# Four edits to a one-core hybrid-decoder kernel: sums of squares by split products with ones, w_o's sums in place, samples' decays weighted half a step sooner, the chunk rows' pool in reverse order

## The chip, the cores and the metric

The kernel runs on one core of one Trainium2 chip. The metric is the device time of the kernel in microseconds; a comparison uses the median of several runs. The engines are named as in the profile: PE (TensorE, the matrix engine) with its weight loads PEld, DVE (VectorE), ACT (ScalarE), POOL (GpSimd) and SP (SyncE, which here issues most of the DMAs). A name with q behind it (SPq, ACTq) is the instruction sequencer of that engine, where DMAs are issued.

## The reference, cut to what matters

One step of a decoder layer for a prompt of 1024 rows and 8 samples of 8 rows, 1088 rows together (T in the kernel):

```python
h = rmsnorm(x, norm_g) * (1 + scale[:, None]) + shift[:, None]
proj = h @ w_in
u_pool, z_pool, z_ssm, xbc, dt_raw, g_raw = jnp.split(proj, SPLITS, axis=-1)
p, pool_new = pool_mix(u_pool, pool_buf, pos0, pool_w, pool_scale)
p = (p * jax.nn.silu(z_pool)) @ w_pool_out
xbc_c, conv_new = causal_conv(xbc, conv_buf, conv_w, conv_b)
y, ssm_new = ssd(xs, dt, A, Bm, Cm, ssm_state)
y = (y + d_skip.astype(jnp.float32)[:, None] * xs).reshape(b, L, D_INNER)
y = rmsnorm(y * jax.nn.silu(z_ssm.astype(jnp.float32)), ssm_norm_g)
s = y.astype(x.dtype) @ w_ssm_out
gates = jax.nn.sigmoid(g_raw)
m = gates[..., :D_MODEL] * p + gates[..., D_MODEL:] * s
x = x + gate[:, None] * (m @ w_o)
```

and in the scan over chunks of 128 rows (`ssd`; the samples take one chunk of 8 rows each, from their own states):

```python
cb = jnp.einsum('bign,bjgn->bijg', Cq, Bq)
att = cb[..., None] * decay * dq[:, None]
y = jnp.einsum('bijge,bjgep->bigep', att, xq)
y = y + jnp.einsum('bign,bige,bgepn->bigep', Cq, jnp.exp(acs), h)
```

D_MODEL is 1024, D_INNER 2048 (DI), with four groups (g) of eight heads of 64 channels and a state of 128. The mean of squares inside the second `rmsnorm` (over the 2048 channels of y, for each row) is what the first of the four edits computes in another way.

## The kernel before, in words

Rows lie along the free axis and channels on the partitions, so a tile of 128 by 1088 holds 128 channels of all rows. A product in float32 is made of three products of split operands: `hi` is the rounded part, `lo` the rest, and hi*hi + hi*lo + lo*hi is summed in PSUM (the names `whi`, `wlo`, `yh`, `yl`). The program runs in stages.

1. Normalisation, the conditioning and the pairs of w_in columns. The pairs use one level of Strassen's scheme (`strassen`, `product`: matmul line L427, DVE additions L436 and L441, weight differences L364, splits on ACT L148 and POOL L151). Beside the last ten pairs runs `all_samples` (L1454 on), a generator that makes the samples' part of the scan, group by group, a step of it between two pieces of the pairs. A step ends at each `yield`.
2. The chunk stage, from about 797 to 1093 us: 32 chunks (four groups of eight, `chunk`), woven with the products by `ph` and by w_ssm_out (`products`, matmul line L235, DVE additions L1828 and L1849) and with `wo_splits`, which prepares w_o for a Strassen product at the end.
3. The tail from 1109 us: sums of squares, the products of the last group (`tail_unit`, `m_done`), and the last products with w_o.

**Order.** Within each engine the instructions run in program order, which the framework's scheduler sets by priorities, except that in the chunk stage PE's and SP's order is the one in which the code is written (`in_line`). So in that stage an edit of tiles or waits can move instructions on DVE, ACT and POOL, and not on PE and SP. Several names are rings: the third R tile of one use waits until the first of an earlier use is free; PSUM is split in rings too: PB for short results, and PA, of three banks, for the blocks of products (`GB`: 384, 352 and 352 rows).

**Samples.** For a group, `rows` scales x by dt into `xd`; `weigh` (L1345) multiplies C and B of all samples (matmul L1349), masks the product (DVE L1351) and multiplies the masked product with the decays into `dec` (DVE L1352); `spread` and `split` make the split operands of the state update (PE L1372, L1374; DVE L1376, L1382, L1385, L1386); `turn` transposes states (L1402); `within` multiplies `dec` with `xd` by the helper `inner` (matmul L1310) and adds D*x.

**Chunks.** Each chunk transposes x and B (L1610, L1612), multiplies B and C (L1613), copies B's transpose to `bt` (ACT L1615), scales x into `xd` (L1621) and `xw` (L1623, one buffer), weights `dec` and `cE` (L1628, L1630), and then multiplies: state update L1635, `inner` L1310 and L1313 (the latter from the state `hst`). `finish` squares the gated result and adds it to `sq_acc`, 128 by 1088, so that a sum over its 128 partitions is the sum of squares. The pool `ck` holds `bt`, `xd`, `xw`, `hst`, `ph` and `szs`; the first tiles asked for of it stand at its lowest addresses (L1814).

**w_o.** `wo_splits` loads for k = 0 to 3 two row blocks of 128 by 1024 of w_o (`up`, `dn`, DMAs L1892 and L1893), forms their differences and sums on DVE (L1900, L1901, L1904, L1905) and splits five results of 512 columns (`part`: ACT copy, POOL difference L1882; stores L1878 and, by `out`, L1887).

**Sums of squares.** For each of nine blocks of rows a matmul with a column of ones gives sums per row on the partitions (L1989); root and reciprocal follow there (L1991, L1992). To bring the result back along the free axis on all partitions, each block becomes a diagonal matrix (DVE L1997) that is multiplied by ones (L1998) into three PSUM banks `rstd`. `m_done` multiplies the gate row tile `r` by them in three pieces (L2047).

Of the kernel before, what the change touches and what calls it, by code (L numbers as in the profile page):

```python
# [46 lines left out]
def tile_pool_ssd_step(  # L47
# [43 lines left out]
    def R(shape=(P, T), dt=F32):  # L91
        return hs.tile(list(shape), dt, tag="R", name=nm("R"), bufs=3)
# [4 lines left out]
    def PB():  # L97
        return psB.tile([P, 512], F32, tag="ps", name=nm("ps"))
# [1351 lines left out]
    def all_samples():  # L1450
# [8 lines left out]
        gs_[0].spread(0)  # L1459
        yield  # L1460
        gs_[0].split(0)
        yield
        for g, m in enumerate(gs_):
            n = gs_[g + 1] if g + 1 < NG else None
            if g:
                gs_[g - 1].end(1)
            m.weigh()
            m.turn(0)
            m.turn(1)
            m.turned(0)  # L1470
# [53 lines left out]
            m.out()  # L1524
            m.update(6)
            m.update(7)
            yield
        gs_[-1].end(1)
        yield
# [281 lines left out]
    cl = open_("cl", 2)  # L1811
    right = tc.tile_pool(name="ck", bufs=2, side="right", reuse_waits="tile")
    ck = right.__enter__()
    for shape, tag, bufs in (((P, 512), "ph", 3), ((P, 512), "hst", 2), ((P, 4, NS), "szs", 1)):  # L1814
        ckt(shape, tag, bufs)

    sq_acc = hs.tile([P, T], F32, tag="sq", name="sq_acc", bufs=1)
# [57 lines left out]
    def wo_splits():  # L1875
# [20 lines left out]
        yield  # L1896
        for k in range(4):
            up, dn = got
            su = R()
            WOE.tensor_tensor(su[:, left_], dn[:, right_], up[:, right_], ALU.subtract)  # L1900
            WOE.tensor_tensor(up[:, right_], up[:, right_], up[:, left_], ALU.subtract)  # L1901
            out()
            yield
            WOE.tensor_tensor(su[:, right_], su[:, left_], up[:, left_], ALU.add)  # L1904
            WOE.tensor_tensor(dn[:, right_], su[:, right_], dn[:, left_], ALU.subtract)  # L1905
            part(oT1, k, up[:, right_])
            yield
            out()
            part(oB11, k, up[:, left_])
            part(oT4, k, dn[:, right_])  # L1910
            yield
            out()
            part(oT3, k, su[:, left_])
            yield
            if k < 3:
                got = rows(k + 1)
            out()
            part(oT2, k, su[:, right_])
            yield
        out()  # L1920
        yield
# [60 lines left out]
        return mp.tile([P, 4, 512], F32R, tag=name, name=name, bufs=1)  # L1982


    rs9 = rs
    ps = PB()
    for c in range(9):
        n = min(P, T - c * P)
        mm(ps[:n, c:c + 1], sq_acc[:, c * P:c * P + n], ones[:, 0:1], start=True, stop=True)  # L1989
    for n, c in ((P, slice(0, 8)), (NS, slice(8, 9))):  # L1990
        act(rs9[:n, c], ps[:n, c], AF.Sqrt, bias=eps[:n], scale=1.0 / DI)  # L1991
        V.reciprocal(rs9[:n, c], rs9[:n, c])  # L1992
    rstd = [PB() for _ in range(3)]
    for c in range(9):
        n = min(P, T - c * P)
        dg = sm.tile([P, P], F32, tag="stc", name=nm("dg"), bufs=4)[:n, :n]
        V.tensor_scalar(dg, ident[:n, :n], rs9[:n, c:c + 1], None, ALU.mult)  # L1997
        mm(rstd[c // 4][:, c % 4 * P:c % 4 * P + n], ones[:n, :], dg, start=True, stop=True)  # L1998

    lo_, up_ = slice(0, 512), slice(512, 1024)
    a11h, a11l, s3h, s3l, s1h, s2h = [part4(n) for n in ("a11h", "a11l", "s3h", "s3l", "s1h", "s2h")]
# [37 lines left out]
    def m_done(m):  # L2042
        r = R()
        load(r, gs_d[m])
        for j, ps in enumerate(rstd):
            s = slice(512 * j, min(512 * j + 512, T))
            V.tensor_tensor(r[:, s], ps[:, :s.stop - s.start], r[:, s], ALU.mult)  # L2047
        mt = M()
        load(mt, m1_d[m])
        a = acc[m]  # L2050

        def done(o, n, ps):
            s = slice(o, o + n)
            V.tensor_tensor(a[:, s], ps[:, :n], a[:, s], ALU.add)
            if m < 7:
                s = slice(0, T)
                if o + n < T:
                    return
            V.tensor_tensor(a[:, s], a[:, s], r[:, s], ALU.mult)
            V.tensor_tensor(a[:, s], a[:, s], mt[:, s], ALU.add)  # L2060
        return done
# [262 lines left out]
```

## Time and profile before

| what | value |
|---|---|
| runs (3) | 1259.56, 1262.73, 1265.03 us; median 1262.73 |
| profiled execution, its own time | 1257.42 us |
| its span in the profile | 1255.7 us |
| mean granted clock of PE | 0.999 |
| PE busy | 1237.1 us, 99% |
| DVE busy | 964.7 us, 77% |
| ACT busy | 671.2 us, 53% |
| POOL busy | 715.3 us, 57% |
| DMA | 257.53 MB, mean 205 GB/s |

A row of a timeline gives the start in us from the start of the span, how long the piece took, the engine, the source line and operation, the tiles written and read, the shape, how many instructions are taken together, and in brackets the idle time just before with what ended it. Matmuls overlap, so the time of a row of several is not the distance to the next row: the distance between two starts is what they cost. A row of the waits names the engine and line that waited, what for, and then the total in us, how often, and the longest. A row of a line gives the number of instructions and the shortest, middle and longest duration in ns. A row of windows gives, for a stretch, the busy time of PE, PEld, DVE, ACT and POOL in this order, each with its number of instructions, then PE's clock, the DMA share and GB/s.

### The profile page before, as it was taken

The numbers are of one execution on the slowest core, as the hardware profiler recorded it, in microseconds if no ns is written. First come the engines' busy times: TensorE is split into PE (matmuls) and PEld (weight loads), VectorE is DVE, ScalarE is ACT, GpSimd is POOL, SyncE is SP. The second block draws the span as 40 slices with busy tenths as digits, with TensorE's granted clock in tenths as the row PEclk, the third lists the DMA queues.
The fourth block names the chain that finished last, engine by engine and source line by source line (L and its number), as shares of the span: only waits on it lengthen the run. The fifth ranks groups of instructions, "written<-read, shape, count | busy, mean of one in ns | idle before, by whom it ended". The sixth has DMA issues, their size and how long they took to land.

```text
span 1255.7 us, 26515 instructions
## 1 busy us (share of the span) xinstructions
PE 1237.1 (99%) x9733; PEld 1159.4 (92%) x9733; DVE 964.7 (77%) x1709; ACT 671.2 (53%) x1542; POOL 715.3 (57%) x607
## 2 busy tenths in 40 slices
PE   9999999999999999999999999999999999999997
PEld 8889999999999999999999999989888888999885
DVE  6993888877988688886666665588677888659986
ACT  6864366555656566546444443656676656402425
POOL 1137768775968677654443334355576777503662
PEclk9999999999999999999999999999999999999999
DMA  9946355474546544435566564998788877866884
GB/s 321 314 139 214 118 177 182 138 223 136 182 155 203 164 153 158 160 112 155 149 188 179 161 197 142 329 310 277 239 249 271 288 242 250 284 228 216 247 197 156
DMA packets 262715, 257.53 MB, mean 205 GB/s; under 512 B 27993, under 2 KB 202345, under 8 KB 262578
## 3 DMA queue, kind: packets, MB, share of 16 engines
q1 hardware_dynamic: 181856, 163.49, 42.5%
q10 hardware_dynamic: 78426, 88.16, 20.3%
q0 software_dynamic: 2304, 4.20, 1.9%
q8 instruction: 77, 1.26, 0.4%
q14 instruction: 52, 0.43, 0.1%
HBM read 170.80 MB, written 85.10 MB: 204 GB/s over the span
## 4 chain that ended last, share of the span: by engine, by line
PE 65%; DVE 3%; DMA 2%; POOL 1%; issue 1%; ACT 1%; SPq 0%; DVEq 0%; POOLq 0%; ACTq 0%
PE mm L235 16%; PE mm L427 14%; PE ps L427 14%; PE ps L1310 2%; PE pc L427 2%; PE pc L1635 2%; PE ps L1313 2%; PE ps L2119 2%; PE ps L2121 2%; PE ps L2120 2%; PE ps L1402 1%; DMA xb<-xbc 1%; PE ps L1425 1%; PE ps L1610 1%; PE pc L1416 1%
## 5 line engine op out<-in xcount | busy, mean ns | idle before, releaser
L151 POOL TENSOR_TENSOR wlo<-rawA,whi 128x512 fp32r<-128x512 f32 x120 | 172.3, 1440 | 118.9 <-ACT whi L148 108.0
L151 POOL TENSOR_TENSOR wlo<-raw,whi 128x512 fp32r<-128x512 f32 x90 | 153.2, 1711 | 89.6 <-ACT whi L148 83.9
L235 PE MATMUL mm<-Y,whi 128*128 128x352 f32 (+1 forms) x960 | 196.5, 334 | 1.8 <-DVE R L1828 1.1
L235 PEld LDWEIGHTS mm<-Y,whi 128*128 128x128 f32 x960 | 159.1, 188 | 8.6 <-issue 4.5
L1148 DVE SCALAR_TENSOR_TENSOR GA<-GA,cvT,GA 128x1112 f32<-128x1112 f32 x72 | 134.4, 1871 | 0.1
L148 ACT ACTIVATE whi<-rawA 128x512 fp32r<-128x512 f32 x120 | 75.3, 628 | 83.9 <-PE ps L427 48.5
L427 PE MATMUL mm<-Y,whi 128*128 128x272 f32 x800 | 119.9, 292 | 0.0
L427 PE MATMUL ps<-Y,whi 128*128 128x272 f32 x800 | 117.7, 289 | 0.0
L427 PEld LDWEIGHTS mm<-Y,whi 128*128 128x128 f32 x800 | 107.8, 188 | 2.7 <-issue 0.9
L148 ACT ACTIVATE whi<-raw 128x512 fp32r<-128x512 f32 x90 | 56.0, 628 | 100.9 <-DVE raw L364 44.3
L427 PEld LDWEIGHTS ps<-Y,whi 128*128 128x128 f32 x800 | 106.7, 188 | 0.3
L235 PE MATMUL mm<-Y,wlo 128*128 128x352 f32 (+1 forms) x480 | 98.7, 327 | 0.0
L1298 ACT ACTIVATE dec<-dec,acT 128x128 f32<-128x128 f32 x256 | 78.7, 389 | 28.4 <-POOL dec L1294 28.4
L235 PEld LDWEIGHTS mm<-Y,wlo 128*128 128x128 f32 x480 | 81.7, 188 | 0.0
L302 POOL TENSOR_TENSOR pw<-pw,ph 128x512 fp32r<-128x512 f32 x40 | 66.2, 1655 | 12.0 <-ACT ph L300 10.9
L427 PE MATMUL mm<-G,whi 128*128 128x272 f32 x480 | 70.9, 289 | 0.0
L427 PE MATMUL ps<-G,whi 128*128 128x272 f32 x480 | 70.5, 289 | 0.0
L427 PE MATMUL mm<-Y,wlo 128*128 128x272 f32 x400 | 66.7, 288 | 0.0
L427 PE MATMUL ps<-Y,wlo 128*128 128x272 f32 x400 | 66.5, 288 | 0.0
L427 PEld LDWEIGHTS mm<-G,whi 128*128 128x128 f32 x480 | 64.4, 189 | 0.7
L427 PEld LDWEIGHTS ps<-G,whi 128*128 128x128 f32 x480 | 64.2, 188 | 0.4 <-issue 0.4
L1572 POOL TENSOR_TENSOR Y<-xb,Y 128x512 fp32r<-128x512 f32 x32 | 41.6, 1301 | 35.6 <-ACT Y L1570 35.6
(593 smaller groups left out, 3244.8 us busy)
## 6 DMA issues: line engine op xcount, KB each, us to landing
rawA<-in_w_in SPq DMA_DIRECT2D x62, 512.0 KB
dec<-acs_d SPq DMA_DIRECT2D x32, 512.0 KB
xbc<-GA ACTq DMA_DIRECT2D x24, 512.0 KB
Y<-wo SPq DMA_DIRECT2D x10, 1024.0 KB
pw<-in_w_ssm_out ACTq DMA_DIRECT2D x32, 256.0 KB
ws<-ph ACTq DMA_DIRECT2D x32, 256.0 KB
ws<-pw ACTq DMA_DIRECT2D x32, 256.0 KB
h<-in_state_ssm SPq DMA_DIRECT2D x32, 256.0 KB
```

Of the source, the lines that this page charges most:

```text
L148: ins = act(hi[:, :, :ncols], raw[:, :, :ncols], AF.Copy)
L151: (eng or nc.gpsimd).tensor_tensor(lo[:, :, :ncols], raw[:, :, :ncols], hi[:, :, :ncols].bitcast(F32), ALU.subtract)
L235: mm(ps[:, :n], w[k // 4][h][:, k % 4, :], r[k][:, o:o + n], start=(j == 0), stop=(j == len(terms) - 1))
L302: nc.gpsimd.tensor_tensor(raw.bitcast(F32R), raw, hi.bitcast(F32), ALU.subtract)
L427: mm(p, w[j // 8][:, k], A(k, s)[j // 4 == 1], start=(j == 0), stop=(j == 11))
L1148: V.scalar_tensor_tensor(d[:, :n], rp[:, k:k + n], cvT[:, 24 * k + mc:24 * k + mc + 1], d[:, :n], ALU.mult, ALU.add)
L1298: act(dec[:, h], dec[:, h], AF.Exp, bias=acT[:, c, 8 * g + h:8 * g + h + 1], scale=-1.0)
L1310: mm(o[hh], xd[:S, 2 * q + hh, :], dec[:S, 2 * q + hh], start=True, stop=state is None)
L1313: mm(o[hh], state[:, h * 64:h * 64 + 64], cE[:, h], start=False, stop=True)
L1572: nc.gpsimd.tensor_tensor(yl[g][:, :, o:o + S], v, yhc.bitcast(F32), ALU.subtract)
L1635: mm(pu, bt, xw.rearrange("p h d -> p (h d)"), start=True, stop=True)
L2119: mm(ps, hi, y[:, k, c0:c0 + cw], start=(first and k == 0), stop=False)
```

## The change

```diff
         gs_[0].split(0)
+        gs_[0].weigh()
         yield
         for g, m in enumerate(gs_):
             n = gs_[g + 1] if g + 1 < NG else None
             if g:
                 gs_[g - 1].end(1)
-            m.weigh()
             m.turn(0)
...
             m.update(6)
             m.update(7)
+            if n:
+                n.weigh()
             yield
...
-    for shape, tag, bufs in (((P, 512), "ph", 3), ((P, 512), "hst", 2), ((P, 4, NS), "szs", 1)):
+    for shape, tag, bufs in (((P, P), "bt", 2), ((P, 8, 64), "xd", 2), ((P, 8, 64), "xw", 1), ((P, 512), "ph", 3),
+                             ((P, 4, NS), "szs", 1), ((P, 512), "t2", 1), ((P, 512), "hst", 2)):
         ckt(shape, tag, bufs)
...
             up, dn = got
-            su = R()
-            WOE.tensor_tensor(su[:, left_], dn[:, right_], up[:, right_], ALU.subtract)
+            WOE.tensor_tensor(dn[:, right_], dn[:, right_], up[:, right_], ALU.subtract)
             WOE.tensor_tensor(up[:, right_], up[:, right_], up[:, left_], ALU.subtract)
             out()
             yield
-            WOE.tensor_tensor(su[:, right_], su[:, left_], up[:, left_], ALU.add)
-            WOE.tensor_tensor(dn[:, right_], su[:, right_], dn[:, left_], ALU.subtract)
+            t2 = ckt([P, 512], "t2", 1)
+            WOE.tensor_tensor(t2, dn[:, right_], up[:, left_], ALU.add)
+            WOE.tensor_tensor(dn[:, left_], t2, dn[:, left_], ALU.subtract)
             part(oT1, k, up[:, right_])
             yield
             out()
             part(oB11, k, up[:, left_])
-            part(oT4, k, dn[:, right_])
+            part(oT2, k, t2)
             yield
             out()
-            part(oT3, k, su[:, left_])
+            part(oT4, k, dn[:, left_])
             yield
             if k < 3:
                 got = rows(k + 1)
             out()
-            part(oT2, k, su[:, right_])
+            part(oT3, k, dn[:, right_])
             yield
...
-    rs9 = rs
-    ps = PB()
-    for c in range(9):
-        n = min(P, T - c * P)
-        mm(ps[:n, c:c + 1], sq_acc[:, c * P:c * P + n], ones[:, 0:1], start=True, stop=True)
-    for n, c in ((P, slice(0, 8)), (NS, slice(8, 9))):
-        act(rs9[:n, c], ps[:n, c], AF.Sqrt, bias=eps[:n], scale=1.0 / DI)
-        V.reciprocal(rs9[:n, c], rs9[:n, c])
-    rstd = [PB() for _ in range(3)]
-    for c in range(9):
-        n = min(P, T - c * P)
-        dg = sm.tile([P, P], F32, tag="stc", name=nm("dg"), bufs=4)[:n, :n]
-        V.tensor_scalar(dg, ident[:n, :n], rs9[:n, c:c + 1], None, ALU.mult)
-        mm(rstd[c // 4][:, c % 4 * P:c % 4 * P + n], ones[:n, :], dg, start=True, stop=True)
+    sq_h = mp.tile([P, T], F32R, tag="sq_h", name="sq_h", bufs=1)
+    act(sq_h, sq_acc, AF.Copy)
+    sq_l = M(dt=F32R)
+    nc.gpsimd.tensor_tensor(sq_l, sq_acc, sq_h.bitcast(F32), ALU.subtract)
+    ones_r = sm.tile([P, P], F32R, tag="stc", name=nm("ones_r"), bufs=4)
+    act(ones_r, ones, AF.Copy)
+    rstd = mp.tile([P, T], F32, tag="rstd", name="rstd", bufs=1)
+    for o, n in GB:
+        ps = PB()
+        mm(ps[:, :n], ones_r, sq_h[:, o:o + n], start=True, stop=False)
+        mm(ps[:, :n], ones_r, sq_l[:, o:o + n], start=False, stop=True)
+        act(rstd[:, o:o + n], ps[:, :n], AF.Sqrt, bias=eps, scale=1.0 / DI)
+        V.reciprocal(rstd[:, o:o + n], rstd[:, o:o + n])
...
-        for j, ps in enumerate(rstd):
-            s = slice(512 * j, min(512 * j + 512, T))
-            V.tensor_tensor(r[:, s], ps[:, :s.stop - s.start], r[:, s], ALU.mult)
+        V.tensor_tensor(r, rstd, r, ALU.mult)
```

The lines of the changed kernel stand two to three higher or lower than those of the kernel before: L1621 becomes L1623, L1849 becomes L1852, L2047 becomes L2044.

**Samples.** On DVE, for the first group, this stood around L1351 and L1352 before the change:

```order
L1382 TENSOR_TENSOR dec_8348<-xw_8346,dec_8348 32x512
L441 TENSOR_TENSOR s_1357_8190<-s_1357_8190,ps_8370 128x272
L364 TENSOR_TENSOR raw_8337<-raw_8336,rawA_8182 128x512
L441 TENSOR_TENSOR u_1359_8192<-u_1359_8192,mm_8395 128x272
L441 TENSOR_TENSOR u_1359_8192<-u_1359_8192,ps_8410 128x272
L364 TENSOR_TENSOR rawA_8184<-rawA_8184,rawA_8182 128x512
L1351 TENSOR_TENSOR ps_8445<-ps_8445,maskS 64x64
L1352 TENSOR_TENSOR dec_8444<-dS_8222,ps_8445 64x8x64
L1397 TENSOR_TENSOR xd_8466<-ps_8471,xd_8466 128x4x64
```

and this stands there now:

```order
L1376 TENSOR_TENSOR xw_8346<-ps_8339,wd_7535 96x512
L1351 TENSOR_TENSOR ps_8356<-ps_8356,maskS 64x64
L1385 TENSOR_TENSOR bt_8351<-ps_8344,bt_8351 32x128
L441 TENSOR_TENSOR s_1357_8190<-s_1357_8190,mm_8360 128x272
L1352 TENSOR_TENSOR dec_8355<-dS_8222,ps_8356 64x8x64
L1386 TENSOR_TENSOR dec_8348<-bt_8351,blk_7536 96x512
L1382 TENSOR_TENSOR dec_8348<-xw_8346,dec_8348 32x512
L441 TENSOR_TENSOR s_1357_8190<-s_1357_8190,ps_8375 128x272
L364 TENSOR_TENSOR raw_8337<-raw_8336,rawA_8182 128x512
```

L1351 and L1352 have moved up past three of the additions L441 and two weight differences L364; L1397, which adds the result of `inner`, stays.

**w_o, third row block (k = 2).** On DVE, before the change; `G` is the sum of a product, `xb`, `xw`, `xd` and `hst` are the chunks':

```order
L1849 TENSOR_TENSOR G_12819<-mm_13900,G_12819 128x384
L1621 TENSOR_TENSOR xd_13927<-ps_13916,dtT 128x512
L1900 TENSOR_TENSOR R_13878<-R_13767,R_13766 128x512
L1901 TENSOR_TENSOR R_13766<-R_13766 128x512
L1904 TENSOR_TENSOR R_13878<-R_13878,R_13766 128x512
L1849 TENSOR_TENSOR G_12819<-mm_13933,G_12819 128x352
L1905 TENSOR_TENSOR R_13767<-R_13878,R_13767 128x512
L1623 TENSOR_TENSOR xw_13929<-ps_13916,wdT 128x512
L1643 TENSOR_TENSOR hst_13966<-hst_13966,pc_13947 128x512
```

and now:

```order
L1632 TENSOR_TENSOR cE_13743<-cE_13743,ps_13804 128x1024
L1902 TENSOR_TENSOR R_13771<-R_13771,R_13770 128x512
L1650 SCALAR_TENSOR_TENSOR xb_13510<-xb_13510,Dv,ps_13832 128x128 x4
L1852 TENSOR_TENSOR G_12637<-mm_13885,G_12637 128x352
L1903 TENSOR_TENSOR R_13770<-R_13770 128x512
L1907 TENSOR_TENSOR t_2351_14000<-R_13771,R_13770 128x512
L1570 TENSOR_TENSOR xb_13510<-xb_13510,sz_13678 128x512
L1852 TENSOR_TENSOR G_12823<-mm_13903,G_12823 128x384
L1623 TENSOR_TENSOR xd_13930<-ps_13919,dtT 128x512
L1908 TENSOR_TENSOR R_13771<-t_2351_14000,R_13771 128x512
L1852 TENSOR_TENSOR G_12823<-mm_13936,G_12823 128x352
L1625 TENSOR_TENSOR xw_13932<-ps_13919,wdT 128x512
```

The first sum now stands behind `cE` of the chunk before, and one of the four instead of all four stands between `xd` and `xw` of the same chunk. For k = 1 the first sum has moved from behind `cE` of a chunk to behind `xw` of the one before, for k = 3 from behind `xd` to behind `hst` of the one before; for k = 0 it stays.

**The tail.** On DVE after the last addition of the chunk stage, now (`mm_15223`, `mm_15237` and `mm_15251` are the first three blocks of the last group's product, one bank of PA each):

```order
L2000 RECIPROCAL rstd<-rstd 128x384
L2000 RECIPROCAL rstd<-rstd 128x352 x2
L2051 TENSOR_TENSOR G_12255<-mm_15223,G_12255 128x384
L2051 TENSOR_TENSOR G_12255<-mm_15237,G_12255 128x352
L2051 TENSOR_TENSOR G_12255<-mm_15251,G_12255 128x352
L2044 TENSOR_TENSOR R_15218<-rstd,R_15218 128x1088
L2044 TENSOR_TENSOR R_15276<-rstd,R_15276 128x1088
L2044 TENSOR_TENSOR R_15334<-rstd,R_15334 128x1088
```

Before, two reciprocals of 8 columns and of one, and four L1997, stood ahead of the first of these additions. On PE the nine matmuls L1989 and the nine L1998 are gone, and six of 384 or 352 columns stand in front of the last group's first product.

## The prediction

> **What bounds the kernel now.** I read the share of busy time first, then the waits of TensorE, then the timelines of PE, DVE, ACT and SP around each place the change touches.
>
> ```profile
> PE 1237.1 (99%) x9733; PEld 1159.4 (92%) x9733; DVE 964.7 (77%) x1709; ACT 671.2 (53%) x1542; POOL 715.3 (57%) x607
> ...
> PE ps L1310 <- DVE dec L1352: 2.3, 2, 1.3
> PE ps L1612 <- DVE xw L1623: 1.5, 2, 1.4
> PE mm L235 <- DVE R L1828: 1.1, 1, 1.1
> ...
> PE ps L1313 <- POOL R L1882: 0.7, 1, 0.7
> ```
>
> PE is busy for 1237.1 of 1255.7 us, so only 18.6 us of the span are not matmul. The change can gain in two ways: it takes matmuls away, or it takes away a wait in which PE stood. The four waits above (2.3 + 1.5 + 1.1 + 0.7 = 5.6 us) are the ones at the places that the diff touches. DVE, ACT and POOL count only where PE waits for them.
>
> **Samples' decays (weigh).** The two waits at L1310 are those of the first and the third group of samples.
>
> ```profile
> 597.62 0.68 DVE L1352 TENSOR_TENSOR dec<-dS,ps 64x512 f32<-64x512 f32 x1
> ...
> 598.36 0.68 PE L1310 MATMUL ps<-dec,xd 64*64 64x64 f32 x16 [1.27 <-DVE dec L1352]
> ...
> 687.17 0.68 PE L1310 MATMUL ps<-dec,xd 64*64 64x64 f32 x16 [1.01 <-DVE dec L1352]
> ```
>
> DVE writes `dec` up to 598.30, and PE's L1310 starts right behind it. Nothing is added: the same matmul L1349, the same small product L1351 and the same 0.68 us L1352 on DVE, four times each. In the new order L1349 stands at least 24 matmuls sooner, and L1351 and L1352 stand ahead of the DVE additions that they stood behind. So `dec` is ready before PE comes to L1310, and 1.27 + 1.01 = 2.28 us go. What can be late next is `xd` or the transposed states, which before were ready while PE waited. The price of the edit is that L1351 and L1352, under 1 us together, now delay additions whose banks PE needs: at half of that for each of the four groups it would be +2.0. Bounds -2.28 to +2.0; I take -2.28, because DVE, busy for 77% of the span, was the late one here only by its order.
>
> **The chunk rows' pool.** The first chunk's `bt`, `xd` and `xw` lie, before, over buffers of the last pair of columns, whose stores are still going.
>
> ```profile
> 797.59 0.33 ACTq L518 DMA_DIRECT2D gs<-u  x1
> ...
> 801.71 0.28 ACT L1615 ACTIVATE bt<-ps 128x128 f32<-128x128 f32 x1 [4.15 <-DMA gs<-u]
> ...
> 797.01 2.48 DVE L1673 TENSOR_TENSOR Y<-Y,Y 128x1088 fp32r<-128x1088 f32 x2
> 803.16 0.69 DVE L1621 TENSOR_TENSOR xd<-ps,dtT 128x512 f32<-128x512 f32 x1 [3.67 <-DMA gs<-u]
> ...
> 804.37 1.41 DVE L1828 TENSOR_TENSOR R<-mm,R 128x384 f32<-128x384 f32 x3
> ...
> 804.97 0.97 PE L235 MATMUL mm<-Y,whi 128*128 128x384 f32 x4 [1.14 <-DVE R L1828]
> ...
> 812.96 0.58 ACT L1639 ACTIVATE hst<-pc 128x512 f32<-128x512 f32 x1
> ```
>
> DVE's `xd` waits 3.67 us for such a store, the additions L1828 queue behind it, and PE waits 1.14 us for a bank. After the change these three tiles lie over the raw weight rows, which were read long before, and `hst`, which takes their place, is first written at 812.96, long behind the last of these stores. `xd` can start when L1673 ends (799.5), 3.67 us sooner, more than the 1.14 that PE lost. Bounds -1.14 to 0 (another tile of the pool waits for a store in its place); I take -1.14.
>
> **w_o's sums in place.** Four DVE sums of 512 columns for each of four row blocks stay, the splits and stores stay, PE's order stays. What goes is the third R tile: the sum L1900 no longer waits for its earlier stores.
>
> ```profile
> 902.41 0.43 SPq L1893 DMA_DIRECT2D R<-in_w_o  x1
> ...
> 909.31 0.76 DVE L1900 TENSOR_TENSOR R<-R,R 128x512 f32<-128x512 f32 x1 [4.01 <-DMA R<-in_w_o]
> ...
> 1005.32 1.08 DVE L1900 TENSOR_TENSOR R<-R,R 128x512 f32<-128x512 f32 x1 [3.00 <-DMA xb<-xbc]
> ...
> 1009.38 0.68 DVE L1623 TENSOR_TENSOR xw<-ps,wdT 128x512 f32<-128x512 f32 x1
> ...
> 1010.11 0.33 PE L1612 MATMUL ps<-ident,bc 128*128 128x128 f32 x1 [1.37 <-DVE xw L1623]
> ```
>
> DVE stood 3.00 us at L1900 at 1005.32; the load named is not its operand, and a store from the third tile's earlier use is what fits. All four sums then stood ahead of `xw`, and PE paid 1.37; the rest of that line's 1.5 and the 0.7 for L1882 (the split of the third tile) belong to the same sums: 2.2 us can go. But the freed sums are put about one chunk sooner, behind the rows below, while the loads of their rows keep their place in SP's hand-written order.
>
> ```profile
> 947.95 0.43 SPq L1893 DMA_DIRECT2D R<-in_w_o  x1
> 955.02 0.69 DVE L1623 TENSOR_TENSOR xw<-ps,wdT 128x512 f32<-128x512 f32 x1
> ...
> 991.32 0.43 SPq L1893 DMA_DIRECT2D R<-in_w_o  x1
> 997.65 1.21 DVE L1630 TENSOR_TENSOR cE<-cE,ps 128x1024 f32<-128x1024 f32 x1
> ...
> 1038.13 0.42 SPq L1893 DMA_DIRECT2D R<-in_w_o  x1
> 1041.76 0.68 DVE L1643 TENSOR_TENSOR hst<-hst,pc 128x512 f32<-128x512 f32 x1
> ```
>
> The load issued at 902.41 let the sum start at 909.31, 6.9 us later. With that, rows are there at 954.85, 998.2 and 1045.0, and the DVE positions behind which the sums now stand end at about 955.7, 998.8 and 1042.4. So two sums would wait little or not at all, and the last about 2.6 us (up to 4.7 if DVE runs ahead, as it may without the old stalls). What queues behind it is `dec` and `cE` of the next chunk, and PE waits for these at L1310 only when the whole of DVE's lead is spent; at 909 a 4.01 us wait cost PE nothing. Where the lead is under a microsecond, such a wait comes through. Bounds: -2.2 (all covered) to +4 (the last wait and two late `xw` come through). I take -0.4, because the chunks of blocks 1 and 2 are also newly woven and about 1.8 us of new small waits would give back most of the 2.2.
>
> **Sums of squares.** Matmuls go from PE, and a long reciprocal comes to DVE.
>
> ```profile
> 1109.12 2.05 PE L1989 MATMUL ps<-ones,sq_acc 128*128 128x1 f32 x18
> 1111.09 0.97 PE L235 MATMUL mm<-Y,whi 128*128 128x384 f32 x4
> 1111.90 0.85 PE L235 MATMUL mm<-Y,wlo 128*128 128x384 f32 x4
> ...
> 1115.36 1.05 PE L1998 MATMUL ps<-dg,ones 128*128 128x128 f32 x8
> 1116.17 0.73 PE L235 MATMUL mm<-Y,whi 128*128 128x352 f32 x3
> ...
> L1212 DVE RECIPROCAL h<-h x1: 1946/1946/1946, 548.8 to 548.8; 128x288 f32<-128x288 f32 x1
> L1992 DVE RECIPROCAL rs<-rs x2: 155/179/203, 1111.5 to 1111.6; 128x8 f32<-128x8 f32 x1, 64x1 f32<-64x1 f32 x1
> ...
> 1111.20 0.41 ACT L1991 ACTIVATE rs<-ps,eps 128x8 f32<-128x8 f32 x2 [18.86 <-PE ps L1989]
> 1119.94 0.60 POOL L2098 TENSOR_TENSOR selS<-ident 128x64 f32<-128x64 f32 x2 [27.20 <-PE ps L1998]
> ...
> L1673 POOL TENSOR_TENSOR Y<-Y,Y x2: 2541/2548/2554, 786.7 to 789.3; 128x1088 fp32r<-128x1088 f32 x2
> ```
>
> PE: the first sums take 1109.12 to 1111.09, 1.97 us; the diagonal spread takes 1115.36 to 1116.17 twice and half of that once, 2.0 us. Six matmuls come, 384 or 352 columns wide; four of 384 take 1111.09 to 1111.90, so 0.20 us each or less: 1.1 us. PE saves 2.9. The copy and the difference ahead of them, 1088 columns each, lie in the 18.86 and 27.20 us in which ACT and POOL wait for nothing else; without that cover POOL's difference alone would put 2.5 us ahead of the sums (L1673 is the same operation).
>
> DVE: reciprocals over 1088 columns. 288 columns took 1.946 us and 8 took 0.203, so 6.2 ns a column and 2.5 + 2.35 + 2.35 = 7.2 us. By the order all three stand ahead of DVE's first addition of the tail. Sums end at 1110.1, the first root is there at about 1110.2, the reciprocals end at 1117.4. PE's blocks of 1.9 to 2.0 us start at 1110.1 and fill the three banks by 1115.9; the fourth needs the first addition (0.56 us), which ends at 1117.9. PE waits 2.0 us there. If only a part of the columns is slow, less; bounds 0.5 to 3.5. Net of this edit: -2.9 + 2.0 = -0.9.
>
> From here DVE has 7.2 us more to do, less 0.4 for the old reciprocals and less nine L1997 of 128 columns, some 0.27 each (a little over a quarter of L1621's 0.69 for 512): about 4.4. R, three pieces before, becomes one of about 1.25 (L1673 on DVE, two of 1088 columns in 2.48); I count that as equal.
>
> ```profile
> 1111.00:1130.00 19.00, 19.00 (x120) 18.70 (x121) 14.34 (x30) 1.04 (x3) 2.16 (x3) 1.00 0.88 320
> 1130.00:1172.00 42.00, 42.00 (x238) 39.93 (x237) 40.11 (x62) 9.81 (x21) 16.45 (x12) 1.00 0.66 220
> ...
> 1128.12 1.56 POOL L2024 TENSOR_TENSOR a11l<-G,a11h 128x512 fp32r<-128x512 f32 x1 [7.59 <-ACT a11h L2023]
> ...
> L2033 DVE TENSOR_TENSOR s<-G x4: 675/978/1787, 1128.5 to 1146.3; 128x512 f32<-128x512 f32 x4
> ```
>
> DVE is idle 4.7 us in the first and 1.9 us in the second of these stretches (third busy column), 6.6 in all, and starts some 1.3 us sooner; 4.4 us more just fit. But R's `rstd` now lies in SBUF, not in PSUM. L2033, two SBUF inputs, took 1.79 us at 1128.5, beside POOL's L2024, and 0.68 at its shortest: +1.1. Eight R's, five of them where POOL works 16.45 of 42 us, could cost DVE 0 to 5.5 us; I take 1 to 2, which the rest of the cover still holds, so 0 on PE.
>
> The Trainium skill, "SBUF — State Buffer", section "SBUF: two separate sides", says that a VectorE operation with two SBUF inputs and a GpSimd operation that reads SBUF exclude each other on a shared port pair for the whole instruction. It speaks against moving `rstd` out of PSUM; the row of L2033 agrees, and by the rule each of the eight R's could wait out a POOL instruction of about 1.5 us, 12 us on DVE at the worst, which is the second rival below at its hardest.
>
> **Sum.** -2.28 - 1.14 - 0.4 - 0.9 = -4.7 on the profiled execution's own 1257.42 us (span 1255.7), so 1252.7. That execution lies 5.3 us under the median of the runs, 1262.73, and below the lowest, 1259.56. Carried to the median: 1258.0 us, 0.37% less.
>
> **Rivals.**
> 1. Every gain and no stall: the scheduler's cover holds, the fourth bank is free in time, and blocks 1 to 3 of w_o cost nothing: -2.28 - 1.14 - 2.2 - 2.9 = -8.5, so 1254. For it: at 909 a 4.01 us wait of DVE cost PE nothing. Against it: three banks, 7.2 us of reciprocals.
> 2. DVE becomes the bound of the tail: R's share of waits for POOL (5.5) on top of 4.4 us in 6.6 us of idle time. Then about 2 to 4 us come out at the end of the stage, where DVE is already busy without a gap, and the total is -2 or -1: 1261.
> 3. Slower: the w_o sums, a chunk sooner, stand before their rows have landed. DVE would wait 3.5, 0.5 and 4.7 us at the three later blocks if it runs about 3 us ahead of the times above, with `xw` of the next chunks behind them, and PE waits there at L1612 as it did at 1010.11, for all of it: +8.7, less the other edits' 4.3, is +4.4, so 1267. It decides once DVE's lead at these chunks is under the wait. For it: the 1.37 and 0.7 us above show that the lead does run out. Against it: PE would have to pay each wait in full.
> 4. The weigh and pool edits do not do what they say, since the next operand is late at the same place: -0.4 - 0.9 alone, so 1261.
>
> **How the numbers follow.** My forecast, -3 to -6.3: 0.50. Rival 1: 0.18. Rival 2: 0.12. Rival 3: 0.10. Rival 4: 0.10. The likeliest one's own range is 1256.4 to 1259.7, to which the scatter of a median of runs adds about 2 us at both ends (the three runs lie 5.5 us apart). The range goes to rival 1 with that scatter, 1251, and up to rival 3, 1267. About what a measurement here can tell from no change is 0.5%, 6.3 us. Faster by more: rival 1 (0.18) and the lower edge of the forecast with scatter (0.12), 0.30. Slower by more: the hard end of rival 3 and what I have not seen, 0.10. Within: 0.60.
>
> **What would show it.** No wait of PE at L1310 for `dec` near 598 and 687; no wait for `gs<-u` on ACT and DVE near 800 and none of PE at 805; on DVE three reciprocals of 2.3 to 2.6 us, and on PE one wait of about 2 us some 6 us behind the last sum of squares; R at about 1.25 us, longer beside POOL. At w_o's sums waits for `in_w_o` at the fourth block. I am wrong if PE waits for `xw` by more than 2 us between 945 and 1060, if the reciprocals stall PE by over 3.5 us, or if PE waits anywhere behind 1130.

## The result, and the profile after

| kernel | runs | median us | ratio to the kernel before, with its 95% interval |
|---|---|---|---|
| before | 22 | 1260.45 (1256.90 to 1265.03) | |
| the change | 22 | 1262.60 (1259.41 to 1264.52) | 1.0017 [1.0009, 1.0026] |

The change made the kernel slower by 0.17%, about 2.1 us, where 0.37% faster was forecast. The profiled execution of the change took 1261.8 us (span 1260.1), that of the kernel before 1257.42 (span 1255.7): 4.4 us between the two spans. The 22 runs of the kernel before have a median 2.3 us under that of its first three.

The page of the change, and then the waits of its PE:

```profile
span 1260.1 us, 26422 instructions
PE 1237.0 (98%) x9703; PEld 1158.3 (92%) x9703; DVE 970.3 (77%) x1685; ACT 673.2 (53%) x1545; POOL 722.6 (57%) x608
...
PE ps L1612 <- DMA xb<-xbc: 5.7, 2, 4.6
PE mm L235 <- DVE G L2051: 2.2, 3, 1.5
```

PE's busy time is the same (1237.0 and 1237.1 us) though some 3 us of matmuls are gone, which says that other matmuls became longer. The waits for `dec` at L1310, for `xw`, and for R of L1828 are no longer in the list; two others have come: for a load of `xb`, 5.7 us, and for DVE's additions in the tail, 2.2 us. The 0.7 us at L1313, put down to POOL's L1882 before and to its L1574 now, stays.

**The start of the chunk stage** in the change, timelines of ACT, DVE and PE:

```profile
797.14 0.28 ACT L1617 ACTIVATE bt<-ps 128x128 f32<-128x128 f32 x1 [0.46 <-ACT u L516]
...
796.13 2.48 DVE L1675 TENSOR_TENSOR Y<-Y,Y 128x1088 fp32r<-128x1088 f32 x2
798.53 0.68 DVE L1623 TENSOR_TENSOR xd<-ps,dtT 128x512 f32<-128x512 f32 x1
...
598.53 0.68 PE L1310 MATMUL ps<-dec,xd 64*64 64x64 f32 x16
...
804.88 0.60 PE L1612 MATMUL ps<-ident,xb 128*128 128x128 f32 x4
```

L1310 has no wait in brackets any more (0.21 us at L1374, at 686 us, is new), `bt` and `xd` follow at once, and PE takes up the second chunk at 804.88. In the kernel before it did so at 807.16, though this execution of the change had been 1.4 us later at L596 (353.05 against 351.60), by scattered waits for first loads.

**The chunk stage** of the change, timelines of POOL, SP and PE, SP's waits between 1004 and 1020, and the windows of PE (length, busy time with its number of matmuls, granted clock, DMA share, GB/s):

```profile
1002.75 2.99 POOL L1885 TENSOR_TENSOR R<-R,ph 128x512 fp32r<-128x512 f32 x2 [0.72 <-ACT ph L1883]
...
1010.31 0.74 POOL L1575 TENSOR_TENSOR sz<-sz 128x256 f32<-128x256 f32 x1
1010.99 2.55 POOL L1885 TENSOR_TENSOR R<-R,ph 128x512 fp32r<-128x512 f32 x2
1015.42 0.48 POOL L1580 TENSOR_TENSOR sz<-sz 128x128 f32<-128x128 f32 x1
1017.77 0.88 POOL L1581 TENSOR_TENSOR sq_acc<-sq_acc,sz 128x128 f32<-128x128 f32 x2
...
1004.07 0.51 SPq L1599 DMA_DIRECT2D xb<-xbc  x1
1018.26 0.53 SPq L1609 DMA_DIRECT2D sz<-z  x1
1020.93 0.46 SPq L1599 DMA_DIRECT2D xb<-xbc  x1
...
1028.10 1.09 PE L1612 MATMUL ps<-ident,xb 128*128 128x128 f32 x4 [4.63 <-DMA xb<-xbc]
SPq L1609 <- POOL sq_acc L1581: 9.0, 1, 9.0
SPq L1609 <- DMA wo<-ph: 5.1, 1, 5.1
...
1028.00:1033.00 5.00, 4.90 (x19) 0.50 1.09 383
1034.00:1038.00 4.00, 4.00 (x43) 1.00 0.54 191
```

Read it from POOL. The first half of a chunk's sum of squares (L1575) is done at 1011.05, but the rest (L1580, L1581) waits behind two more of w_o's differences and the next chunk's L1574 and L1575, and is done only at 1018.2. Until then the chunk's `sz` buffer is in use, one of three. SP stands at its next load of `sz` from 1004.6 to 1018.26, a wait of which the trace puts the first 5.1 us down to a store of w_o and the last 9.0 to L1581, and behind it in SP's hand-written order stands the load of `xb`, which is issued at 1020.93 and is there at 1028.1. PE stood for it for 4.63 us. And after the wait its clock is at 0.50 for about 5 us: four transposes of 1.09 us instead of 0.60.

The order of instructions on POOL says why. Before the change, in this place (xb_13506 is the chunk whose sum it is):

```
L1572 TENSOR_TENSOR Y_13236<-xb_13506,Y_13235 128x4x128
L1573 TENSOR_TENSOR sz_13674<-sz_13674 128x256
L1578 TENSOR_TENSOR sz_13674<-sz_13674 128x128
L1579 TENSOR_TENSOR sq_acc<-sq_acc,sz_13674 128x128
L1641 TENSOR_TENSOR hst_14071<-hst_13966,Elb 128x512
L1882 TENSOR_TENSOR R_13766<-R_13766,ph_13999 128x512
```

and in the change (the same chunk is xb_13510):

```
L1885 TENSOR_TENSOR t_2351_14000<-t_2351_14000,ph_14113 128x512
L1574 TENSOR_TENSOR Y_13240<-xb_13510,Y_13239 128x4x128
L1575 TENSOR_TENSOR sz_13678<-sz_13678 128x256
L1885 TENSOR_TENSOR R_13771<-R_13771,ph_14237 128x512
L1885 TENSOR_TENSOR R_13771<-R_13771,ph_14363 128x512
L1574 TENSOR_TENSOR Y_13240<-xb_13618,Y_13239 128x4x128
L1575 TENSOR_TENSOR sz_13797<-sz_13797 128x256
L1580 TENSOR_TENSOR sz_13678<-sz_13678 128x128
```

The end of the chunk's sum (L1578 and L1579 before, L1580 and L1581 now) stood ahead of all five differences; now it stands behind all five.

**The tail** of the change, timelines of DVE and PE:

```profile
1113.90 6.98 DVE L2000 RECIPROCAL rstd<-rstd 128x384 f32<-128x384 f32 x3 [0.44 <-ACT rstd L1999]
...
1130.00 2.38 DVE L2056 TENSOR_TENSOR G<-G,R 128x1088 f32<-128x1088 f32 x1
...
L2044 DVE TENSOR_TENSOR R<-rstd,R x8: 1275/1282/1443, 1122.1 to 1159.9; 128x1088 f32<-128x1088 f32 x8
...
1112.74 0.33 PE L1997 MATMUL ps<-sq_h,ones_r 128*128 128x384 f32 x1
1113.74 0.86 PE L235 MATMUL mm<-Y,whi 128*128 128x384 f32 x4
1121.34 0.97 PE L235 MATMUL mm<-Y,whi 128*128 128x384 f32 x4 [1.52 <-DVE G L2051]
1148.82 1.90 PE L235 MATMUL mm<-Y,whi 128*128 128x352 f32 x8
...
1156.11 1.90 PE L235 MATMUL mm<-Y,whi 128*128 128x352 f32 x8
```

Six matmuls cost 1.0 us (1112.74 to 1113.74), the reciprocals 6.98. PE waits 1.52 us at the fourth block, and then again and again up to 1156. The rows at 1148.82 and 1156.11 take 1.74 us from first to next, eight matmuls that elsewhere take 1.29: a wait of 0.45 us hides inside each. Adding up what each row takes over its usual pace gives 1.68 + 0.27 + 0.64 + 0.45 + 0.39 + 0.45 = 3.9 us. From the first sum to the first product with `sh`, the samples' part of the next stage (L2126, L2129 before), PE needed 63.7 us, against 63.0 in the kernel before.

### The profile page after: what moved, and what is told of

Read it like the earlier page. It is cut to its first block, busy times and chain, and to the rows that moved or that the text cites. A ratio compares the mean times of both kernels' runs of the same rounds, so it can differ in the third digit from the quotient of the medians.

```text
span 1260.1 us, 26422 instructions
## 1 busy us (share of the span) xinstructions
PE 1237.0 (98%) x9703; PEld 1158.3 (92%) x9703; DVE 970.3 (77%) x1685; ACT 673.2 (53%) x1545; POOL 722.6 (57%) x608
## 4 chain that ended last, share of the span: by engine, by line
PE 62%; DVE 5%; DMA 3%; issue 1%; POOL 1%; ACT 0%; SPq 0%; DVEq 0%; ACTq 0%; POOLq 0%
PE mm L427 14%; PE ps L427 14%; PE mm L235 13%; PE ps L1310 2%; PE pc L427 2%; PE pc L1637 2%; PE ps L1313 2%; PE ps L2118 2%; PE ps L2116 2%; PE ps L2117 2%; DMA R<-in_w_o 1%; PE ps L1402 1%; DMA xb<-xbc 1%; PE ps L1612 1%; PE ps L1425 1%
## 5 line engine op out<-in xcount | busy, mean ns | idle before, releaser
L1574 POOL TENSOR_TENSOR Y<-xb,Y 128x512 fp32r<-128x512 f32 x32 | 41.2, 1290 | 42.0 <-ACT Y L1572 42.0
```

The costliest lines, as they stand in the source:

```text
L1574: nc.gpsimd.tensor_tensor(yl[g][:, :, o:o + S], v, yhc.bitcast(F32), ALU.subtract)
```

## The experiments

Eleven kernels ran, 6 to 12 times each, against the kernel before on the same chip. An interval reaches some 1 to 2 us to either side.

| what | median us | before, us | ratio, 95% interval |
|---|---|---|---|
| change, w_o's sums as before | 1257.50 | 1261.58 | 0.9978 [0.9963, 0.9992] |
| change, four sz buffers | 1257.97 | 1261.58 | 0.9971 [0.9961, 0.9982] |
| change, sums of squares as before | 1264.13 | 1261.58 | 1.0022 [1.0009, 1.0035] |
| change, filler matmuls | 1263.93 | 1261.58 | 1.0022 [1.0013, 1.0031] |
| before, w_o edit alone | 1266.60 | 1260.81 | 1.0045 [1.0032, 1.0058] |
| before, sums edit alone | 1261.01 | 1260.81 | 1.0001 [0.9989, 1.0013] |
| change, reciprocal root on ACT | 1260.29 | 1260.81 | 0.9996 [0.9988, 1.0005] |
| change, four sz and root on ACT | 1256.51 | 1260.81 | 0.9958 [0.9942, 0.9974] |
| before, weigh and pool alone | 1257.91 | 1260.64 | 0.9975 [0.9964, 0.9986] |
| weigh, pool, sums with root on ACT | 1255.45 | 1260.64 | 0.9955 [0.9938, 0.9972] |
| before, one-column sums twice | 1264.43 | 1260.64 | 1.0034 [1.0020, 1.0047] |

### 1. The w_o edit undone

```diff
-            WOE.tensor_tensor(dn[:, right_], dn[:, right_], up[:, right_], ALU.subtract)
+            su = R()
+            WOE.tensor_tensor(su[:, left_], dn[:, right_], up[:, right_], ALU.subtract)
...
```

> The change with w_o's sums as before (third R tile back), the other three edits kept. Theory A: the new 4.63 us wait of PE for an xb load at 1028 and the 1.05 at 1076 come from the w_o edit, because POOL now does w_o's five differences ahead of the chunk's sum of squares, so the sz buffer is late and SP stands at the sz load with the xb load behind it. Then both waits go, the half-speed stretch behind the first (about 2.4 us) goes with it, and the old waits of about 2.2 us come back: 1262.6 - 4.6 - 2.4 - 1.1 + 2.2 = 1256.7 us. Theory B: PE waits there only because the weigh and pool edits let it run 3.4 us ahead of its loads; then the wait stays and the time is 1261 to 1263.

Measured 0.9978. PE's timeline has no wait for `xb` of 0.2 us or more; what is left in the chunk stage is the old kind, for `xw` (and 0.53 us near 910):

```profile
1008.29 0.37 PE L1614 MATMUL ps<-ident,bc 128*128 128x128 f32 x1 [2.28 <-DVE xw L1625]
1008.74 1.63 PE L235 MATMUL mm<-Y,whi 128*128 128x384 f32 x4
...
1054.60 0.33 PE L1614 MATMUL ps<-ident,bc 128*128 128x128 f32 x1 [0.53 <-DVE xw L1625]
```

PE is still 3.4 us ahead by the other two edits and its loads are in time. So running ahead is not what made `xb` late; the w_o edit is (theory A). But the old wait has a price of its own here: behind its 2.28 us the clock is at 0.50 from 1008.44 to 1011.85, so that the four matmuls at 1008.74 take 1.42 us to the next row instead of 0.78. In the profiled execution of the kernel before, 1.37 us at this place did not do that.

### 2. Four sz buffers

```diff
-        sz = ckt([P, 4, P], "sz", 3)
+        sz = ckt([P, 4, P], "sz", 4)
...
-            hi = ck.tile([P, 512], F32R, tag="ph", name=nm("ph"), bufs=3)
+            hi = ck.tile([P, 512], F32R, tag="ph", name=nm("ph"), bufs=2)
```

> The change with four sz buffers instead of three (and two ph buffers instead of three, to make room). Theory A: SP no longer stands at the sz load, xb is there in time, and PE loses none of 4.6 + 2.4 + 1.1: about 1254.5 us, no wait of PE for xb over 0.5 us. If the load itself or the DMA traffic is what is late (theory B), the waits stay and the time is 1261 to 1263.

Measured 0.9971, and the loads come as they should. SP and PE of this run:

```profile
1006.47 0.46 SPq L1599 DMA_DIRECT2D xb<-xbc  x1
1007.02 0.52 SPq L1609 DMA_DIRECT2D sz<-z  x1
1014.12 0.42 SPq L1599 DMA_DIRECT2D xb<-xbc  x1
1017.80 0.52 SPq L1609 DMA_DIRECT2D sz<-z  x1
...
1024.59 0.60 PE L1612 MATMUL ps<-ident,xb 128*128 128x128 f32 x4
1054.65 0.33 PE L1614 MATMUL ps<-ident,bc 128*128 128x128 f32 x1 [2.35 <-DVE xw L1625]
```

`sz` follows 0.6 us behind `xb` instead of 14 us, and the next `xb` is issued 10 us before PE asks for it. All four edits are in this kernel, and with one more `sz` buffer and one `ph` buffer less the loss is gone: it is the hold of SP at the `sz` load that made it. (With the other rings the scheduler also puts the chunk's sum ahead of the last of the five differences. But L1581 ends at 1017.77 here, hardly sooner than the 1018.2 of the change, and what it still holds is the `sz` load after the next `xb`, at 1017.80: it is the fourth buffer, not the new order, that let `xb` go at 1014.12.) The time is 3.5 us over what was expected, 2.3 us by the ratios. A wait for `xw` of 2.35 us came at the fourth row block, where DVE stood 3.41 us at the first sum for the load of w_o's rows and did the others ahead of `xw`; one of 1.71 us came in the tail.

### 3. The sums of squares as before

```diff
-    sq_h = mp.tile([P, T], F32R, tag="sq_h", name="sq_h", bufs=1)
-    act(sq_h, sq_acc, AF.Copy)
...
+    for c in range(9):
+        n = min(P, T - c * P)
+        mm(ps[:n, c:c + 1], sq_acc[:, c * P:c * P + n], ones[:, 0:1], start=True, stop=True)
...
```

> The change with the sums of squares as before. If the tail costs what the trace shows (+0.8 us from the end of the chunk stage to the first product with sh), this is 0.8 us faster than the change: 1261.8, and PE has no wait for DVE between 1110 and 1172. If the forecast's -0.9 had been right, it would be 1263.5.

Measured 1.0022, against the change's 1.0017 and 0.8 us less expected, so undoing the edit did not help. PE has no wait for DVE there, as expected, but its windows show something else (busy time, granted clock, DMA share, GB/s):

```profile
1117.44 2.05 PE L1992 MATMUL ps<-ones,sq_acc 128*128 128x1 f32 x18
...
1121.42 2.55 PE L235 MATMUL mm<-Y,whi 128*128 128x384 f32 x8
...
1117.00:1119.00 2.00, 2.00 (x19) 1.00 0.44 53
1120.50:1123.50 3.00, 3.00 (x11) 0.50 1.05 403
```

Behind the nine one-column sums the clock goes to 0.50 for 3.4 us (1120.31 to 1123.72), though PE never waited there; eight matmuls take 2.4 us instead of 1.3. From the first sum to the first product with `sh` this run needs 64.5 us. In the profiled execution of the kernel before, the same code kept its clock (63.0). So the old sums have a cost that comes in some executions only. Experiment 11 asks for it.

### 4. Fillers while PE waits

```diff
         px = PB()
+        for _ in range(22 if (g, c) == (3, 2) else 0):
+            mm(px[:, :P], ident, ident, start=True, stop=True)
```

> The change with 22 idle matmuls of the identity with itself ahead of the transposes of the chunk whose xb is late, so that PE is busy while it waits. If the half-speed matmuls from 1028 to 1033 come from PE having been idle, the clock stays at 1.0 and the time falls by about 2.4 us, to 1260.2, though xb lands when it did. If they come from the DMA traffic at that time, the clock row still shows 0.5 and the time stays at 1262.6 or a little above.

Measured 1.0022, no gain against the change's 1.0017: the mechanism was right and the time was not. A window and the timeline of PE:

```profile
1028.00:1033.00 5.00, 5.00 (x41) 1.00 1.10 381
...
1025.36 5.08 PE L1612 MATMUL ps<-ident 128*128 128x128 f32 x44
1030.36 0.66 PE L1614 MATMUL ps<-ident,xb 128*128 128x128 f32 x4
1036.14 0.44 PE L1310 MATMUL ps<-dec,xd 128*64 128x128 f32 x4
1077.54 0.66 PE L1614 MATMUL ps<-ident,xb 128*128 128x128 f32 x4 [2.20 <-DMA xb<-xbc]
```

With as much DMA traffic as before (a share of 1.10), the clock stays at 1.00: the half speed comes from PE's idleness, not from the traffic. The chunk takes 5.8 us from its transposes to L1310, against 8.1 in the change (1028.10 to 1036.22). But the fillers put the transposes 0.2 us later than the wait had done (5.64 against 5.43 us behind the start of the last row ahead of them), and the next wait for `xb` is 2.20 instead of 1.05 us: what PE gains it waits for later. From that row to the transposes at 1077.54 this trace gains 0.5 us on the change, not 2.4. Why the next load is no sooner was not tested.

### 5. The w_o edit alone

The kernel before with the change's `wo_splits`, and `t2` in `ck`.

> The kernel before with w_o's sums in place and nothing else changed. Theory A (POOL does w_o's differences ahead of the chunk's sums, SP stands at the sz load, xb is late): the whole chain moves along with PE, so the wait for xb of about 4.6 us, the half-speed stretch behind it (2.4) and a second wait of about 1 us are here too, less the old waits of 2.2: 5 to 6 us slower than the kernel before. If the wait also needs PE to be 3.4 us ahead by the weigh and pool edits, only about 1.2 us of it is left, PE stays at full clock, and the time is within 1.5 us of the kernel before.

Measured 1.0045, 5.8 us slower, within theory A. The wait and the clock are there without the other edits:

```profile
1035.63 1.09 PE L1610 MATMUL ps<-ident,xb 128*128 128x128 f32 x4 [5.43 <-DMA xb<-xbc]
...
1035.00:1038.50 3.50, 2.87 (x12) 0.51 1.04 368
```

### 6. The sums edit alone

The kernel before with the new sums and the one `m_done` line.

> The kernel before with the new sums of squares and nothing else changed. PE saves 3.0 us of matmuls and waits for DVE behind the reciprocals (1.5 us) and at later blocks, 3.7 us in all: against an execution of the kernel before that keeps its clock, +0.8 us. The nine one-column sums, in which the array does next to nothing for 2 us, are gone; if they are what halves PE's clock for 3.3 us in part of the executions (1.6 us lost, as in the run with the old sums), then the mean gains some 0.8 us by that, and the two cancel: within 1 us of the kernel before, with the clock row at 1.0 in the tail.

Measured 1.0001 [0.9989, 1.0013], as expected. The waits for DVE at 1120, 1146 and 1153 (1.52, 0.52 and 0.24 us) are those of the change. All 12 runs have a mean clock of 0.997 or more; the kernel before, beside the first four experiments, had 30 runs: 16 at 0.998 or more with a median of 1260.2 us, and 14 below with 1262.1. Beside this experiment, on another chip, it had 23: 14 with 1260.6 and 9 with 1261.1.

### 7. The reciprocal root on ACT

```diff
-        act(rstd[:, o:o + n], ps[:, :n], AF.Sqrt, bias=eps, scale=1.0 / DI)
-        V.reciprocal(rstd[:, o:o + n], rstd[:, o:o + n])
+        act(rstd[:, o:o + n], ps[:, :n], AF.Ln, bias=eps, scale=1.0 / DI)
+    for o, n in GB:
+        act(rstd[:, o:o + n], rstd[:, o:o + n], AF.Exp, scale=-0.5)
```

> The change with the reciprocal root formed on ACT (exponential of minus half the logarithm) in place of root on ACT and reciprocal on DVE. If DVE's 7.0 us of reciprocals is what PE pays for in the tail (3.7 us of waits and hidden waits), these waits go and the time falls by about 3.3 us against the change, to a ratio of about 0.999 to the kernel before. If R with two SBUF inputs beside POOL is what makes DVE late, the waits at 1146 and 1154 stay and only the 1.5 us behind the reciprocals goes.

Measured 0.9996. In the tail one wait of PE is left:

```profile
1119.26 3.70 DVE L2045 TENSOR_TENSOR R<-rstd,R 128x1088 f32<-128x1088 f32 x3 [0.83 <-ACT rstd L2001]
...
1156.32 0.97 PE L235 MATMUL mm<-Y,whi 128*128 128x384 f32 x4 [0.65 <-DVE G L2052]
```

From the first sum to the first product with `sh` it is 60.4 us, 3.3 less than in the change: exactly the expected amount in the trace, and 2.6 us (0.21%) by the ratios. R still has two SBUF inputs here, and the waits at 1147 and 1154 are gone. So it was the 7 us of reciprocals, not the port, that PE paid for.

### 8. Both cures

Experiments 2 and 7 together, all four edits kept.

> Four sz buffers and the reciprocal root on ACT together, all four edits kept. If both losses are what the runs so far say, they add up: 0.9971 of the run with four sz buffers less 3.3 us (0.0026) gives a ratio of about 0.9945, 1254.5 us or a little above, faster than both kernels.

Measured 0.9958 [0.9942, 0.9974], 1256.51 us: faster than both kernels. The expected 0.9945 lies within the interval. The largest wait that is left in the chunk stage is the one for `xw` at 1056 (2.38 us), as in experiment 2.

### 9. Weigh and pool alone

```diff
+        gs_[0].weigh()
...
-            m.weigh()
...
+                             ((P, 4, NS), "szs", 1), ((P, 512), "hst", 2)):
```

> The kernel before with only the weigh edit and the pool's order. If these two are worth what the trace of the change shows at its start (2.28 + 1.14 us of PE's waits gone, nothing late in their place), it is 3.4 us faster than the kernel before, ratio 0.9973. If PE, 3.4 us ahead, waits in the chunk stage for loads that come no sooner, the gain shrinks to under 1.5 us and the trace shows waits of PE for xb or xw there that the kernel before does not have.

Measured 0.9975, 2.7 us; the expected 0.9973 lies within the interval. No new wait is there at 598 or 805, and one of 0.20 us at 687. The wait for `xw` in the fourth row block is 0.98 us instead of 0.17, but that is no price of these edits: experiments 6 and 11, whose code up to there is that of the kernel before, show 1.84 and 1.94 us at this place.

### 10. The three other edits, with the root on ACT

Experiment 1 with the reciprocal root of experiment 7.

> Weigh, pool order and the new sums with the reciprocal root on ACT; w_o's sums as before. Weigh and pool -3.4, sums -3.0 + 0.7: about 5.7 us faster than the kernel before, ratio 0.9955, less up to 1.5 us for the waits for xw at w_o's third tile, which were 2.8 us in the run without the w_o edit.

Measured 0.9955 [0.9938, 0.9972], 1255.45 us, as expected. It is the lowest ratio of all; the interval does not part it from experiment 8, so nothing here shows that w_o's sums in place are worth having.

### 11. The one-column sums twice

```diff
-        mm(ps[:n, c:c + 1], sq_acc[:, c * P:c * P + n], ones[:, 0:1], start=True, stop=True)
+        for _ in range(2):
+            mm(ps[:n, c:c + 1], sq_acc[:, c * P:c * P + n], ones[:, 0:1], start=True, stop=True)
```

> The kernel before with each of the nine one-column sums of squares done twice, so that PE spends 3.9 us instead of 2.0 in matmuls of one column. Plain cost: +2.0 us. If such matmuls count as next to no work for PE's clock, then 3.9 us of them halve the clock behind them in nearly every execution (over 3.3 us, 1.6 us lost), where 2.0 us do it only in part of them: +2.8 to +3.6 us in all, and the clock row shows 0.5 to 0.65 in the first 4 us behind the sums. If the clock does not depend on them, +2.0 and a clock of 1.0 there.

Measured 1.0034, 3.8 us by the medians and 4.3 by the ratio: a little above the upper end, and the interval leaves +2.0 out. Timeline and windows of PE:

```profile
1113.08 4.81 PE L1990 MATMUL ps<-ones,sq_acc 128*128 128x1 f32 x36
...
1115.00:1117.00 2.00, 2.00 (x15) 0.71 1.00 380
1119.00:1121.00 2.00, 2.00 (x8) 0.50 1.05 386
1123.00:1126.00 3.00, 3.00 (x24) 1.00 1.05 386
```

The clock halves at 1115.85, while the sums still run, and comes back 6.8 us later; 11 of the 12 runs have a mean clock of 0.996 or less.

## Why the prediction was wrong, point by point

**Weigh: right.** -2.28 was forecast. L1310 has no wait, 0.20 us came in its place at 687, and with the pool's order it made 2.7 us (experiment 9), of 3.4 forecast for both.

**The pool's order: right** in the mechanism and the size: `xd` starts at 798.53, directly behind L1675, and the second chunk 2.3 us sooner.

**w_o's sums: wrong, and this is the step that turned the sign.** The working said "the splits and stores stay, PE's order stays" and followed the sums on DVE alone, with bounds of -2.2 to +4 and -0.4 taken. Alone the edit costs 5.8 us (experiment 5), in the change 1.0017 against 0.9978 without it (experiment 1), 4.9 us. DVE's new waits for the loads were small, 0.58 us at the second row block and 1.17 at the fourth, and PE paid nothing for them. What it paid for is one engine further: with the sums sooner, their splits are sooner on POOL, ahead of a chunk's sum of squares, and that sum holds an `sz` buffer for which SP stands, with the `xb` load queued behind it. The rival that ended on the slower side had the right edit and sign (+4.4 us in all), but put the price on `xw` at L1612, and it was given 0.10; its own mechanism shows only in experiments 2 and 8, once in each, with 3.41 and 3.80 us on DVE and 2.35 and 2.38 on PE. Its waits (3.5, 0.5 and 4.7 us) do not follow from the times given, either: rows at 954.85, 998.2 and 1045.0, and positions 3 us ahead of 955.7, 998.8 and 1042.4, make 2.2, 2.4 and 5.6. The 2.2 us that were to go were read from one execution, and 0.7 of them, the wait at L1313, did not go with the third tile: it stands with the edit too, in the change and in experiments 5 and 7. The waits for `xw` were 1.5 us in that trace, and 3.1 and 4.0 in experiments 6 and 11, where the same code runs up to there. The step left out: a moved DVE instruction moves what ACT and POOL do with its result, and whatever stands behind that on POOL.

A second part was in no term: the clock. The wait of 4.63 us itself cost 4.6, and the half speed behind it 2.3 more (8.1 against 5.8 us for the same chunk, experiment 4).

Alone, the edits measured +5.8 (experiment 5), 0.2 (experiment 6) and -2.7 us (experiment 9), together 3.3; all in one kernel made +2.1, which the intervals do not part from that.

**Sums of squares: two terms mis-sized, in opposite directions.** PE's saving (2.9 forecast, 3.0 measured) and the reciprocals (7.2 and 6.98) were right, and the stall behind them 2.0 forecast, 1.7 measured. But "the rest of the cover still holds, so 0 on PE" failed: DVE's 4.4 us of extra work went on to cost PE some 2.2 us at later blocks, up to 1156. So -0.9 became +0.8 in the trace. PE did wait behind 1130 (0.47 us at 1147, 0.23 at 1154), which the prediction had named as a sign that it is wrong. The timed runs show 0 (experiment 6), with an interval that still holds +0.8. What speaks for a true 0 is the other miss: the old sums halved PE's clock in some executions, which the one profiled execution of the kernel before did not show. Leaving out the kernels with the wait for `xb`, 39 of 88 runs with the nine one-column sums (the kernel before beside the experiments, and experiment 9) had a mean clock under 0.998, and 7 of 42 with the new ones (experiments 1, 2, 6, 8 and 10). That this makes up just the difference is not shown, and the sums are not the only reason for a lower clock: experiment 1 shows it behind a wait for `xw`.

**The port rival** was not what happened: R ran 1.28 to 1.44 us in the change. Another row with two SBUF inputs did stretch: seven of L2056, with 1088 columns, took 12.2 us, against 9.4 in the kernel before (L2059), and up to 2.38 each. So some of that rival's price did fall on DVE. But with the reciprocals gone (experiment 7), where R in its turn goes up to 2.38, one wait of PE of 0.65 us is left for these additions.

**The base.** The forecast was set on a median of three runs, 1262.73; 22 runs of the same kernel have 1260.45. The high base hid part of the miss: 1262.60 lies 4.6 us over the forecast 1258.0, but from 1260.45 the same -4.7 leads to 1255.7, and 6.9 us are missing. The sign does not depend on the base. That the time lies within the range is luck: its upper end, 1267, was that of the rival with `xw`, which did not happen in the change.

## What to carry to other kernels

When a scheduler may move an instruction, follow its result through every engine that handles it and ask what now stands behind it there: here a gain on DVE became a hold on SP through a ring of three buffers. Before taking one profiled execution as the base, look at the granted clock of several runs, and at the same wait in several traces: a stretch at half speed in some of them is as large as the edits that are being weighed. A wait of PE can cost more than itself (4.63 us cost 2.3 more at half speed), and an operation that leaves PE for an engine at 95% of its stage is not hidden work.

## What the runs showed of the hardware

PE's granted clock fell to 0.50 behind waits of 4.63 and 5.43 us, and with matmuls in that gap it stayed at 1.00. The length of the wait alone does not decide: 2.28 us brought half speed in experiment 1, and 2.35 and 2.38 us in experiments 2 and 8 did not.

The traces show when it changes. Read with fine windows, each stretch at 0.50 ahead of the end is 3.4 or 6.8 us long (the change and experiments 1, 3, 5, 7 and 11), and within one execution all changes lie on a grid of 3.413 us: in the change 1026.39, 1033.21 and, behind the last matmul, 1255.08, which is 2 and 65 steps. Counted by that grid from 300 us on, each step at full speed with 1.13 us or less of matmuls was followed by half speed, and none with 1.60 us or more, one-column sums aside. So it matters how a wait lies on the grid: in experiment 1 the 2.28 us fell wholly into one step, in experiment 2 only 1.78 of the 2.35 us did.

The Trainium skill, "TensorE: Matmul & The Clock Gate", section "Part 1: The HAM clock gate (the "warmup" mystery)", says that the clock halves after an idle window of about 3.4 us, free-running, and comes back after a busy one of that length. The grid here agrees with the length and with its running free. The window need not be wholly idle, by these traces: that of experiment 1 had 1.13 us of matmuls in it.

Matmuls of one column, in which the profile shows PE as busy throughout, were not enough to keep the clock: the doubled sums halved it while they ran, and the 2.0 us of the single ones did so in experiment 3, and not in the kernel before and experiments 5 and 9. The grid fits that too, if these matmuls count as none: in experiment 3 all of the 1.97 us lie in one step, with 1.44 us of other matmuls, and in the other three executions at most 1.67 us do.
